# Attention pairs in a hybrid block: where the keys' sums, the two-group scores and the weighings stand in the order of the engines

## The chip, the cores and the metric

The kernel runs on one core of a Trainium2 chip. The metric is the device time of one execution in microseconds (us). A core has several engines, each with its own instruction order, which wait for one another through semaphores: TensorE (PE, matrix products), VectorE (DVE), ScalarE (ACT), GpSimd (POOL), and SyncE (SP), whose queue issues most of the transfers.

## The reference

Two layers on 512 tokens of width 1024, in float32: one dilated attention mixer and one mLSTM mixer, each followed by a feed-forward part. The change is in the attention (and, by one address, in a projection of the mLSTM). Cut to that:

```
xn = rms_norm(x, g)
proj = (xn @ w_in)                      # 3 groups x (q, k, v) x 8 heads of 128
for (window, dilation) in ((128, 1), (512, 4), (2048, 16)):     # groups 0, 1, 2
    q, k = rope(q) * scale, rope(k)     # only the first 32 of the 128 dimensions are turned
    s = q @ k^T within blocks of 128 and the block before, masked
    o, lse = softmax(s) @ v, log-sum-exp of s
o = sum over groups of softmax(lse) * o
out = o @ w_out
```

## The kernel before

The heads are worked on in four pairs (`pr` 0 to 3; tiles `a0...` to `a3...`), and each pair has three groups g0, g1, g2. `qk_unit` makes the queries and keys of one pair and group (256 columns each) by seven products in the order P1, P5, P6, P2, P7, P3, P4, in the manner of a fast matrix multiplication: sums of input halves (`S`, `S3`, `S4`) against differences of weight quarters (`less`, L958, on VectorE), and sums of the results. A product is 24 matmuls of 128x256. Float32 accuracy comes from splitting each weight chunk into a high part (`..._h`, cast on ScalarE, L239) and a low part (`..._l`, a subtraction on VectorE, L241); the matmuls go high, high, low for every quarter of the chunk, so that the first two matmuls of a product need only the high part and the third needs the low part. `Feed` issues the splits ahead of the products that use them; `feed.pop` hands out one chunk and issues (`fill`) the next.

After its product, `finish` reads the accumulators: bank copies on ScalarE (`vu`, L1007 after P5 and L1010 after P6; `u` from `c11`, L1045), copies of queries (L1022) after P2 and P4, keys' sums on VectorE (`a.g_k`, L1028) after P7 and P3, and packings of the 32 turned rows (`rot`, L990) on ScalarE. P7 and P4 add to the same accumulator `u`, so that P4 can start only when the keys' sum after P7 has read it. After P4 the rope follows on VectorE (L627 to L636), and the turned rows are copied back by ScalarE (L650) and, after g2, for the keys by POOL (L641).

Meanwhile the previous pair's attention is placed between the products: scores of group 0 (`scores0`, L729, with masked maxima on VectorE, L735), scores of groups 1 and 2 together (`both_groups`, 32 matmuls L791, eight maxima L795), exponentials on ScalarE (L814), the joint weights of the three groups (`joint`, to the factors `cf`, L855), then `weigh(0)` and `weigh(1)`, which scale the 15 probability blocks of each head in eight instructions (L863 on ScalarE, L865 on VectorE), `transposes(i)` (turnings: 2.17 us on VectorE, L878, and four DMAs on POOL's queue, L881), `bring(i)` (one DMA, L886) and `values(i)`.

What sets the order: the program is written out in one order, and each engine then gets its part through a scheduler that may interchange independent instructions by priority. Ticks (`advance`, `defer`) place the work of the previous pair: `RUN_AT` gives the tick of the two-group scores, of the seven steps of `rest` (joint, weigh 0, transposes 0, bring 0, weigh 1, transposes 1, bring 1), of the values and of the loads; `FIRST_AT` holds for the attention of pair 0, that runs in pair 1. `None` in `rest` puts a step behind g1's P7 (`behind_seventh`). `run` lets a step stand ahead; `behind(fn, engine=E)` issues it behind the last instruction so far of that engine. `ahead_of_splits` and `ahead_of_casts` name the instruction behind which the next low parts and casts go. `late` and `run_late` hold low parts back so that they are issued among the score maxima. `TOKENS` is the pair of offsets, inside padded tiles, of the high and low parts of weights for the projections of tokens (`mv`, L330).

Of the kernel before, what the change touches and what calls it, by code (L numbers as in the profile page):

```python
# [24 lines left out]
HEADS = 8  # L25
# [8 lines left out]
C2 = float(np.float32(np.uint32(np.float32(TWO_PI - C1).view(np.uint32) & 0xFFFFF000).view(np.float32)))  # L34
C3 = float(np.float32(TWO_PI - C1 - C2))
SCORES0_AT = 7
RUN_AT = (1, (4, 4.5, 5, 7, 7, 8, 9), (14.4, 15.4), (4, 5, 4))
PRODUCTS_FROM = 1
FIRST_AT = (2, (4, 4.5, None, 7, 7, 8, 9)) + RUN_AT[2:]
LAST_AT = (2, (3,), (), (4, 4, 4))  # L40
STACK_AT = (9, 11, 15, 17)
HEAD_AT = ((9, 10, 12), (10, 11, 13), (12, 13, 15), (13, 14, 16), (15, 16, 18), (16, 17, 19), (18, 19, 21),
           (19, 20, 21))
LAST_OUTPUTS = {6: 22, 7: 23}
W_BUFS = 3
PAD, WIDE, NARROW, TOKENS = 64, (0, 0), (16, 48), (48, 16)
SPLITS = [(0, 0), (0, 1), (1, 0)]


# [27 lines left out]
def tile_hybrid_dilated_attn_mlstm(  # L77
# [66 lines left out]
    def defer(n, fn):  # L144
        later.append((tick[0] + n, next(order), fn))
# [63 lines left out]
    ahead_of_splits = [None]  # L209
# [91 lines left out]
    class Feed:  # L301
# [4 lines left out]
        def __bool__(self):  # L306
            return bool(self.ready or self.plan)

        def pop(self, _=0):
            whl = self.ready.pop(0) if self.ready else self.plan.pop(0)()  # L310
            self.fill(self.ahead)
            return whl

        def fill(self, n):
# [110 lines left out]
    with ExitStack() as actx:  # L425
# [257 lines left out]
        def attention_pair(pr, qks):  # L683
# [35 lines left out]
            def scores0(q, k):  # L719

                inner = True
                for i in range(2):
                    for b2 in range(2):
                        sp = score_bank(i, "%ss0" % nm)
                        o, parts = 0, []
                        for b in (2 * b2, 2 * b2 + 1):
                            lo_ = max(b - 1, 0) * P
                            w = (b + 1) * P - lo_
                            nc.tensor.matmul(sp[:, o:o + w], q[:, i, b * P:(b + 1) * P],  # L729
                                             k[:, i, lo_:lo_ + w], start=True, stop=True)  # L730
                            parts.append((b, o, w))
                            o += w
                        for b, o, w in parts:
                            pb = max(2 * b - 1, 0)
                            nc.vector.tensor_tensor_reduce(  # L735
                                p0[i][:, pb:pb + w // P, :].rearrange("p a b -> p (a b)"),
                                sp[:, o:o + w], mask_band[:, 2 * P - w:], 1.0, -3e38,
                                op0=ALU.add, op1=ALU.max, accum_out=own[:, 0, 0, i, b:b + 1])
                    if inner:
                        behind(negate, 0, i, engine=DVE)  # L740
                        if i and pr:
                            held_exps.append(lambda i=i: exponentials(0, i, False))
                        else:
                            if i:
                                feed.fill(3)
                            exponentials(0, i, False)
                        run_late(i)
                ahead_of_splits[0] = last_on(DVE)

                def exps():  # L750
                    for i in range(2):
                        exponentials(0, i)
                if inner:
                    ahead_of_casts[0] = last_on(ACT)
                else:
                    defer(1, lambda: behind(exps, engine=ACT))
# [101 lines left out]
            def weigh(i):  # L858
                cf4 = weight[0]

                def times(blk, f):
                    if i and pr < HEADS // 2 - 1:
                        nc.scalar.activation(blk, blk, AF.Copy, scale=f)  # L863
                    else:
                        nc.vector.tensor_scalar(blk, blk, f, None, op0=ALU.mult)  # L865
                for b in range(4):
                    pb = max(2 * b - 1, 0)
                    blk = p0[i][:, pb:2 * b + 1, :].rearrange("p a b -> p (a b)")
                    times(blk, cf4[:, 0, i, b:b + 1])
                for c in range(4):  # L870
                    blk = p12[i].rearrange("p (g c) k -> p c g k", g=2)[:, c]
                    times(blk, cf4[:, 1, i, c:c + 1])
# [50 lines left out]
            return (lambda: (places(), scores0(*qks[0])), scores12, rest, values, load_values,  # L923
                    value_tiles, bring, second)

        postponed, behind_seventh = [], []

        QK_ORDER = ("P1", "P5", "P6", "P2", "P7", "P3", "P4")
        four_k = lambda t: t.rearrange("p (k n) -> p k n", k=4)
# [51 lines left out]
        def qk_unit(pr, g, qk, then=None):  # L981
# [57 lines left out]
            for n, name in enumerate(QK_ORDER):  # L1039
                key = target[name]  # L1040
                if name in ("P1", "P5"):
                    acc[key] = acc_tile(nm + key)
                if name == "P5":
                    acc["u"] = acc_tile(nm + "u")
                    nc.scalar.activation(acc["u"], acc["c11"], AF.Copy)  # L1045
                    if g:
                        ahead_of_casts[0] = last_on(ACT)
                    feed.fill(feed.ahead + 1)
                whl = feed.pop()
                with fenced():  # L1050
                    for m in range(2):
                        for k in range(4):
                            for a, b in SPLITS:
                                if name in ("P1", "P2", "P4"):
                                    x_ = pair[b][k + 4 * (name != "P1")][:, HALF * (name == "P4"):HALF * (1 + (name == "P4"))]
                                else:
                                    x_ = sum_part(name, b, k)
                                nc.tensor.matmul(acc[key][:, m * HALF:(m + 1) * HALF], whl[a][:, k, m * P:(m + 1) * P], x_,
                                                 start=(name in ("P1", "P5") and m == 0 and k == 0 and (a, b) == SPLITS[0]),
                                                 stop=(m == 1 and k == 3 and (a, b) == SPLITS[-1]), skip_group_check=True)  # L1060
                finish(name)
                if g == 1 and name == "P7":
                    while behind_seventh:
                        behind(behind_seventh.pop(0), engine=DVE)
                if pr == 0:
                    if g == 1:
                        if n == 0:
                            renew(range(4, 8))
                        elif n < 3:
                            sum_of("S%d" % (n + 2))  # L1070
                        elif n == 6:
                            back = rope(qk, rot, False)
                            defer(1, lambda: behind(back, engine=ACT))
                            for key, hf in (("W11", 1), ("W12", 0), ("W12", 1), ("W22", 0), ("W22", 1)):
                                behind(load_block, 0, key, hf, engine=mybir.EngineType.SP)
                    elif n == 6:
                        postponed.append(lambda: rope(qk, rot, False)())
                    if n in (1, 5):
                        advance()
                    continue  # L1080
                if g == 2 and n == 2:
                    feed.ahead = 2
                if n == 6:
                    with behind_scores() if g == 2 else nullcontext():
                        back = rope(qk, rot, g == 0)
                    if g == 0:
                        defer(1, lambda: back(True))
                    elif g == 2:
                        ahead_of_splits[0] = last_on(DVE)
                        back(True)  # L1090
                        ahead_of_casts[0] = last_on(ACT)
                    else:
                        defer(1, lambda: behind(back, engine=ACT))
                if g == 2 and n == 5:
                    late[0] = last or by_products(pr + 1, 0)
                    feed.fill(feed.ahead + 1)
                    late[0] = False
                if n in (1, 3, 5, 6):
                    advance()
                if n == 6 and then is not None:  # L1100
                    then()
                if n:
                    feed.fill(feed.ahead + 1)
# [289 lines left out]
        def follow(todo, at):  # L1393
            scores12_, rest, values, load = todo[1:5]
            for g in range(3):
                defer(at[3][g], lambda g=g: load(g))
            defer(at[0], lambda: run(scores12_ if at is not LAST_AT else lambda: scores12_((2,))))
            for n, fn in zip(at[1], rest):
                if n is None:
                    behind_seventh.append(fn)  # L1400
                else:
                    defer(n, lambda fn=fn: run(fn) if fn is rest[0] else fn())
            for i in range(len(at[2])):
                defer(at[2][i], lambda i=i: run(lambda: values(i)))
# [1172 lines left out]
```

## Time and profile before

| quantity | value |
|---|---|
| median of 3 runs | 1349.94 us (1349.56 to 1349.94) |
| profiled execution | 1350.34 us, span 1348.6 us |
| TensorE busy | 1329.1 us (99%) |
| VectorE busy | 1131.8 us (84%) |
| ScalarE busy | 812.8 us (60%) |
| POOL busy | 196.6 us (15%) |
| the four attention pairs in the span | about 40 to 400 us |

The span goes from the first to the last instruction; the profiled execution's own time includes what lies around it. A row of a timeline reads: start in us, duration in us, engine, line, operation, tiles written and read, shape, number of instructions in the row, and in brackets the engine's idle time before it with what ended it. Buffer numbers and the product's number are left out in the rows, so that `a3g0P_h` is any high part of pair 3, group 0.

### The profile page before, as it was taken

What the parts mean: (1) busy time and instruction counts of PE and PEld (TensorE: products, weight loads), DVE (VectorE), ACT (ScalarE), POOL (GpSimd) and SP (SyncE); (2) the same over time, 40 slices, a digit from 0 to 9 for tenths busy, and PEclk for the clock granted to TensorE, in tenths of its full rate; (3) what the DMA queues carried; (4) which work ended last, traced back from release to release, by engine and by line L of the source; (5) the groups of instructions that cost most, each with busy time, mean ns of one, the idle gap of its engine ahead of it and who ended that gap; (6) DMA issues with size and microseconds to landing.
All of it is one profiled execution on the core that took longest, in us unless ns stands there. A gap on an engine that the chain in (4) does not pass through costs nothing. (4 is left out here: it accounts for less than half of the span.)

```text
span 1348.6 us, 23346 instructions
## 1 busy us (share of the span) xinstructions
PE 1329.1 (99%) x9100; PEld 1219.9 (90%) x9100; DVE 1131.8 (84%) x1787; ACT 812.8 (60%) x1303; POOL 196.6 (15%) x272
## 2 busy tenths in 40 slices
PE   9999999999999999999999999999999999999997
PEld 7898899999998889999999998898888999999886
DVE  7988789799876399888888899898858988997887
ACT  6676577667674255555577464795534555558855
POOL 3000013141412001000010110122200202112113
PEclk9999999999999999999999999999999999999999
DMA  9354244555676357334362743324343535447863
GB/s 302 129 180 155 80 141 149 164 175 154 185 267 192 128 148 175 107 123 126 125 157 79 172 129 89 100 64 125 95 121 98 130 128 173 141 139 172 190 172 102
DMA packets 141270, 194.90 MB, mean 145 GB/s; under 512 B 9028, under 2 KB 106116, under 8 KB 141160
## 3 DMA queue, kind: packets, MB, share of 16 engines
q1 hardware_dynamic: 120128, 140.73, 33.3%
q0 software_dynamic: 19808, 52.48, 16.1%
q8 instruction: 71, 1.16, 0.4%
q10 hardware_dynamic: 1224, 0.21, 0.1%
q14 instruction: 39, 0.32, 0.1%
HBM read 167.30 MB, written 22.54 MB: 141 GB/s over the span
## 5 line engine op out<-in xcount | busy, mean ns | idle before, releaser
L1803 POOL DMA_DIRECT2D f0S<-in_ffn_w_out_dram x10 | 8.7, 875 | 245.0 <-DVE f0hid L1719 161.8
L2366 POOL DMA_DIRECT2D hD<-hB x32 | 20.7, 654 | 109.4 <-DVE hB L2363 109.2
L1827 POOL DMA_DIRECT2D f1T<-in_ffn_w_out_dram x15 | 17.8, 1186 | 86.1 <-ACT f1T L1830 40.5
L276 PE MATMUL mo<-n_h,mo_k_h 128*128 128x512 f32 x64 | 25.4, 397 | 0.0
L276 PE MATMUL mo<-n_h,mo_k_l 128*128 128x512 f32 x64 | 25.2, 394 | 0.0
L276 PE MATMUL awo<-ao_h,awo_k_h 128*128 128x512 f32 x64 | 25.2, 393 | 0.0
L276 PE MATMUL mo<-n_l,mo_k_h 128*128 128x512 f32 x64 | 25.1, 393 | 0.0
L276 PE MATMUL mwo<-yo_l,mwo_k_h 128*128 128x512 f32 x64 | 25.1, 392 | 0.0
L276 PE MATMUL mqk<-n_h,mqk_k_h 128*128 128x512 f32 x64 | 25.1, 392 | 0.0
L276 PE MATMUL mwo<-yo_h,mwo_k_l 128*128 128x512 f32 x64 | 25.1, 392 | 0.0
L276 PE MATMUL mqk<-n_l,mqk_k_h 128*128 128x512 f32 x64 | 25.1, 392 | 0.0
L276 PE MATMUL f0j<-n_h,f0j_h 128*128 128x512 f32 x64 | 25.0, 391 | 0.0
L276 PE MATMUL f1j<-n_h,f1j_h 128*128 128x512 f32 x64 | 25.0, 391 | 0.0
L276 PE MATMUL mwo<-yo_h,mwo_k_h 128*128 128x512 f32 x64 | 25.0, 391 | 0.0
L276 PE MATMUL mqk<-n_h,mqk_k_l 128*128 128x512 f32 x64 | 25.0, 391 | 0.0
L276 PE MATMUL awo<-ao_h,awo_k_l 128*128 128x512 f32 x64 | 25.0, 391 | 0.0
L276 PE MATMUL awo<-ao_l,awo_k_h 128*128 128x512 f32 x64 | 25.0, 390 | 0.0
L276 PE MATMUL f0j<-n_h,f0j_l 128*128 128x512 f32 x64 | 24.9, 390 | 0.0
L276 PE MATMUL f1j<-n_h,f1j_l 128*128 128x512 f32 x64 | 24.9, 390 | 0.0
L276 PE MATMUL f0j<-n_l,f0j_h 128*128 128x512 f32 x64 | 24.9, 389 | 0.0
L276 PE MATMUL f1j<-n_l,f1j_h 128*128 128x512 f32 x64 | 24.9, 389 | 0.0
L241 DVE TENSOR_TENSOR v1P_l<-v1W,v1P_h 128x1024 fp32r<-128x1024 f32 x14 | 17.1, 1223 | 9.2 <-ACT v1P_h L239 9.1
(2746 smaller groups left out, 5993.4 us busy)
## 6 DMA issues: line engine op xcount, KB each, us to landing
f0j_w<-in_ffn_w_in_dram SPq DMA_DIRECT2D x17, 512.0 KB, 6.0
f1j_w<-in_ffn_w_in_dram SPq DMA_DIRECT2D x17, 512.0 KB, 6.6
f1T<-in_ffn_w_out_dram POOLq DMA_DIRECT2D x15, 512.0 KB, 7.4
f0hid<-in_ffn_w_in_dram SPq DMA_DIRECT2D x9, 512.0 KB, 5.1
f1hid<-in_ffn_w_in_dram SPq DMA_DIRECT2D x9, 512.0 KB, 5.1
v0W<-in_attn_w_in_dram SPq DMA_DIRECT2D x8, 512.0 KB, 8.2
v1W<-in_attn_w_in_dram SPq DMA_DIRECT2D x8, 512.0 KB, 4.3
awo_k_w<-in_attn_w_out_dram SPq DMA_DIRECT2D x8, 512.0 KB, 4.0
```

What stands on the lines that cost most here:

```text
L241: nc.vector.tensor_tensor(lo[:, :n], raw[:, :n], hi[:, :n].bitcast(F32), op=ALU.subtract)
L276: nc.tensor.matmul(acc, whl[a][:, k, m * P:(m + 1) * P], pairs[b][kk], start=(kk == 0 and (a, b) == SPLITS[0]), stop=(kk == nk - 1 and (a, ...
L1803: nc.gpsimd.dma_start(t, src[1][:, ks], accum_op=ALU.add)
L1827: nc.gpsimd.dma_start(view(to), weight_rows(hk * UNITS + u, n), accum_op=ALU.add)
L2366: nc.gpsimd.dma_start(hD[k // 4].rearrange("(b i) x -> i b x", i=R)[:, :, c0:c0 + R], t[R * a_:R * (a_ + 1)])
```

## The change

Six things change.

1. The two-group scores of the previous pair go behind P6 of g0 instead of behind P5, in pairs 2 and 3 (`RUN_AT[0] = None`).
2. `transposes(0)` goes behind g1's P7 in all pairs (in pair 1 it already did), and `weigh(1)` right behind the bank copy of g1's P6 on ScalarE (`-1`).
3. After P7 and P3 of g1 in pairs 1 to 3 the keys' sum is written ahead of the next splits and of the turnings (`sums_first`: `feed.pop` without `fill`).
4. `weigh(0)` of pair 0 moves from VectorE to ScalarE, where 16 weighings then stand in a row in pair 1.
5. At the end of pair 3 one low part is no longer issued among the score maxima of its first half (`run_late(0)`).
6. `TOKENS` becomes (48, 48): the low parts of the mLSTM's token weights lie at another offset.

```diff
-RUN_AT = (1, (4, 4.5, 5, 7, 7, 8, 9), (14.4, 15.4), (4, 5, 4))
+RUN_AT = (None, (4, 4.5, None, 7, -1, 8, 9), (14.4, 15.4), (4, 5, 4))
-FIRST_AT = (2, (4, 4.5, None, 7, 7, 8, 9)) + RUN_AT[2:]
+FIRST_AT = (2, (4, 4.5, None, 7, -1, 8, 9)) + RUN_AT[2:]
-PAD, WIDE, NARROW, TOKENS = 64, (0, 0), (16, 48), (48, 16)
+PAD, WIDE, NARROW, TOKENS = 64, (0, 0), (16, 48), (48, 48)
...
-        def pop(self, _=0):
+        def pop(self, fill=True):
             whl = self.ready.pop(0) if self.ready else self.plan.pop(0)()
-            self.fill(self.ahead)
+            if fill is not False:
+                self.fill(self.ahead)
...
-                        run_late(i)
+                        if i or pr < HEADS // 2 - 1:
+                            run_late(i)
...
-                    if i and pr < HEADS // 2 - 1:
+                    if (i or pr == 0) and pr < HEADS // 2 - 1:
                         nc.scalar.activation(blk, blk, AF.Copy, scale=f)
...
-                whl = feed.pop()
+                sums_first = pr > 0 and g == 1 and name in ("P7", "P3")
+                whl = feed.pop(not sums_first)
...
                 finish(name)
+                if g == 0 and name == "P6":
+                    while scores_behind_sixth:
+                        scores_behind_sixth.pop()()
+                if g == 1 and name == "P6":
+                    while behind_sixth:
+                        behind(behind_sixth.pop(), engine=ACT)
+                if sums_first:
+                    ahead_of_splits[0] = last_on(DVE)
                 if g == 1 and name == "P7":
                     while behind_seventh:
                         behind(behind_seventh.pop(0), engine=DVE)
+                if sums_first:
+                    feed.fill(feed.ahead)
...
-            defer(at[0], lambda: run(scores12_ if at is not LAST_AT else lambda: scores12_((2,))))
+            if at[0] is None:
+                scores_behind_sixth.append(lambda: run(scores12_))
+            else:
+                defer(at[0], lambda: run(scores12_ if at is not LAST_AT else lambda: scores12_((2,))))
             for n, fn in zip(at[1], rest):
                 if n is None:
                     behind_seventh.append(fn)
+                elif n < 0:
+                    behind_sixth.append(fn)
```

What it does to the engines' orders is shown at three places. The names carry their buffer numbers here, and the product's number where it has one; the lines of the changed kernel are one to three higher.

First, ScalarE in pair 1, from the bank copy after g1's P6 on. Before (`a0p0` and `a0p1` are the probabilities of the two heads of pair 0):

```order
L1010 ACTIVATE a1g1vu_2134<-a1g1u_2101 128x512
L239 ACTIVATE a1g1P4_h_2168<-a1g1W21_1920 128x1024
L863 ACTIVATE a0p1_1708<-a0p1_1708,a0cf_2034 128x128
L863 ACTIVATE a0p1_1708<-a0p1_1708,a0cf_2034 128x256 x3
L990 ACTIVATE rot_2198<-a1g1c11_2068 32x512
L1022 ACTIVATE a1g1_q_2066<-a1g1c11_2068 128x2x256
L239 ACTIVATE a1g2P1_h_2201<-a1g2W11_2074 128x1024
L863 ACTIVATE a0p1_1708<-a0p1_1708,a0cf_2034 128x2x128 x4
L990 ACTIVATE rot_2198<-a1g1_k_2067 32x512
L239 ACTIVATE a1g2P5_h_2239<-a1g2W11_2074 128x1024
L990 ACTIVATE rot_2198<-a1g1_k_2067 32x512
```

Now:

```order
L1012 ACTIVATE a1g1vu_2134<-a1g1u_2101 128x512
L239 ACTIVATE a1g1P4_h_2176<-a1g1W21_1920 128x1024
L865 ACTIVATE a0p0_1707<-a0p0_1707,a0cf_2034 128x128
L865 ACTIVATE a0p0_1707<-a0p0_1707,a0cf_2034 128x256 x3
L865 ACTIVATE a0p0_1707<-a0p0_1707,a0cf_2034 128x2x128 x4
L865 ACTIVATE a0p1_1708<-a0p1_1708,a0cf_2034 128x128
L865 ACTIVATE a0p1_1708<-a0p1_1708,a0cf_2034 128x256 x3
L865 ACTIVATE a0p1_1708<-a0p1_1708,a0cf_2034 128x2x128 x4
L992 ACTIVATE rot_2206<-a1g1c11_2068 32x512
L1024 ACTIVATE a1g1_q_2066<-a1g1c11_2068 128x2x256
L239 ACTIVATE a1g2P1_h_2209<-a1g2W11_2074 128x1024
```

The weighings of the first head (`a0p0`), which were VectorE's, and all of the second now stand between P4's high part and the copies after P2; g2's P1 high part stands behind sixteen weighings instead of four.

Second, VectorE in pair 3 at g0, around the low part of P6 (`ISA` rows on `a2s12` are the maxima of the two-group scores). Before:

```order
L636 TENSOR_TENSOR rot_3339<-rot_3339 128x512
L958 TENSOR_TENSOR a3g0W11_3217<-a3g0W22_3288,a3g0W11_3217 128x1024
L958 TENSOR_TENSOR a3g0W12_3254<-a3g0W22_3288,a3g0W12_3254 128x1024
L795 ISA a2p0_3408,a2own_2595<-a2s12_3554,acst_109 128x2x128
L795 ISA a2own_2595 128x1
L241 TENSOR_TENSOR a3g0P6_l_3473<-a3g0W11_3217,a3g0P6_h_3472 128x1024
```

Now:

```order
L637 TENSOR_TENSOR rot_3339<-rot_3339 128x512
L960 TENSOR_TENSOR a3g0W11_3217<-a3g0W22_3288,a3g0W11_3217 128x1024
L960 TENSOR_TENSOR a3g0W12_3254<-a3g0W22_3288,a3g0W12_3254 128x1024
L241 TENSOR_TENSOR a3g0P6_l_3473<-a3g0W11_3217,a3g0P6_h_3472 128x1024
L241 TENSOR_TENSOR a3g0P2_l_3488<-a3g0W21_3346,a3g0P2_h_3487 128x1024
L241 TENSOR_TENSOR a3g0P7_l_3523<-a3g0W12_3254,a3g0P7_h_3522 128x1024
L960 TENSOR_TENSOR a3g0W21_3346<-a3g0W21_3346,a3g0W11_3217 128x1024
L241 TENSOR_TENSOR a3g0P3_l_3555<-a3g0W22_3288,a3g0P3_h_3554 128x1024
L797 ISA a2p0_3408,a2own_2595<-a2s12_3585,acst_109 128x2x128
```

P6's low part, and those of P2, P7 and P3, stand ahead of all maxima; before, the first maximum stood ahead of P6's.

Third, VectorE in pair 3 at g1, from P4's low part on. Before:

```order
L241 TENSOR_TENSOR a3g1P4_l_3950<-a3g1W21_3627,a3g1P4_h_3949 128x1024
L878 STREAM_TRANSPOSE a2pB_3911<-a2p0_3408 128x15x4x32
L241 TENSOR_TENSOR a3g2P1_l_3983<-a3g2W11_3845,a3g2P1_h_3982 128x1024
L1028 TENSOR_TENSOR a3g1_k_3848<-a3g1u_3875,a3g1vu_3908 128x2x256
L958 TENSOR_TENSOR a3g2W11_3845<-a3g2W12_3882,a3g2W11_3845 128x1024
L958 TENSOR_TENSOR a3g2W12_3882<-a3g2W22_3922,a3g2W12_3882 128x1024
L241 TENSOR_TENSOR a3g2P5_l_4014<-a3g2W11_3845,a3g2P5_h_4013 128x1024
L1028 TENSOR_TENSOR a3g1_k_3848<-a3g1p5_3874,a3g1vu_3908 128x2x256
```

Now:

```order
L241 TENSOR_TENSOR a3g1P4_l_3951<-a3g1W21_3627,a3g1P4_h_3950 128x1024
L1030 TENSOR_TENSOR a3g1_k_3848<-a3g1u_3875,a3g1vu_3908 128x2x256
L880 STREAM_TRANSPOSE a2pB_4013<-a2p0_3408 128x15x4x32
L241 TENSOR_TENSOR a3g2P1_l_3984<-a3g2W11_3845,a3g2P1_h_3983 128x1024
L1030 TENSOR_TENSOR a3g1_k_3848<-a3g1p5_3874,a3g1vu_3908 128x2x256
L960 TENSOR_TENSOR a3g2W11_3845<-a3g2W12_3882,a3g2W11_3845 128x1024
L960 TENSOR_TENSOR a3g2W12_3882<-a3g2W22_3915,a3g2W12_3882 128x1024
L628 STREAM_SHUFFLE rot_3980<-rot_3980 128x512
L241 TENSOR_TENSOR a3g2P5_l_4022<-a3g2W11_3845,a3g2P5_h_4021 128x1024
```

The keys' sum after P7 (the first L1028, now L1030) moves ahead of the turnings and of g2's P1 low part, and the sum after P3 ahead of the two differences and of P5's low part. On ScalarE the eight second-head weighings of this pair stand in one row between the bank copy after P6 and P4's high part; before, they stood behind that high part, four before and four behind the copies after P2 and g2's P1 high part.

The order of POOL and of SP's transfers around these places is the same in both kernels.

More of the change, by code (lines that the diff above doesn't have):

```diff
@@ L924, in attention_pair @@
                     value_tiles, bring, second)
-        postponed, behind_seventh = [], []
+        postponed, scores_behind_sixth, behind_sixth, behind_seventh = [], [], [], []
         QK_ORDER = ("P1", "P5", "P6", "P2", "P7", "P3", "P4")
```

## The prediction

> **What bounds the kernel now.** I read the shares first, then TensorE's waits, then the busy time of the stretches that the change touches, and last the timeline of each engine there.
>
> The page gives the shares; the cores' view gives the granted clock:
>
> ```profile
> PE 1329.1 (99%) x9100; PEld 1219.9 (90%) x9100; DVE 1131.8 (84%) x1787; ACT 812.8 (60%) x1303; POOL 196.6 (15%) x272
> core 0: 1348.6 us, clock 0.999
> ```
>
> TensorE is idle for 1348.6 − 1329.1 = 19.5 us of the span. The change removes no matmul, so that idle time is all that an order can win. Its waits, costliest first:
>
> ```profile
> PE a3g1u L1058 <- DVE a3g_k L1028: 1.4, 1, 1.4
> PE a1s L791 <- POOL a1g_k L641: 1.4, 1, 1.4
> PE a2g1u L1058 <- DVE a2g_k L1028: 0.8, 1, 0.8
> PE a1g2u L1058 <- ACT a1g2vu L1010: 0.7, 1, 0.7
> ...
> PE a1g1u L1058 <- DVE a1g_k L1028: 0.7, 1, 0.7
> ...
> PE a3s L771 <- DVE a3own L735: 0.5, 1, 0.5
> ```
>
> Three of them (1.4 + 0.8 + 0.7 = 2.9) are the keys' sums ahead of P4, one is the copy of keys by POOL ahead of the two-group scores, one a bank copy, one the last scores. The engines' load in pair 2 around g1 and g2 (second number TensorE, fourth VectorE, fifth ScalarE):
>
> ```profile
> 275.00:310.00 35.00, 33.61 (x292) 33.05 (x290) 33.69 (x49) 25.60 (x42) 12.63 (x19) 1.00 0.60 186
> ```
>
> In 275 to 310 VectorE is busy 33.69 of 35 us, as much as TensorE. Whatever makes VectorE stand idle there is not made good until the stretch ends. That is the view on which I decide.
>
> **Part 1: two-group scores behind P6 (pairs 2 and 3, g0).** No instruction is added; 32 matmuls and 8 reductions swap places with P6. Pair 3, rows picked from the engines' timelines, one engine after the other (start, duration, both in us), as in the fences below:
>
> ```profile
> 323.82 2.76 DVE L958 TENSOR_TENSOR a3g0W<-a3g0W,a3g0W 128x1024 f32<-128x1024 f32 x2
> 327.19 1.22 DVE L241 TENSOR_TENSOR a3g0P_l<-a3g0W,a3g0P_h 128x1024 fp32r<-128x1024 f32 x1
> 325.31 1.06 ACT L239 ACTIVATE a3g0P_h<-a3g0W 128x1024 fp32r<-128x1024 f32 x1
> 324.04 3.02 POOL L641 COPY a2g_k<-rot 32x512 f32<-32x512 f32 x2 [5.28 <-DVE rot L636]
> 325.08 3.73 PE L791 MATMUL a2s<-a2g_k,a2g_q 128*128 128x128 f32 x32
> 328.57 0.48 PE L1058 MATMUL a3g0u<-S,a3g0P_h 128*128 128x256 f32 x2
> ```
>
> P5 ends at 325.08 and the scores fill TensorE until 328.57, 3.49 us. Under that cover P6's two weight differences (to 326.58), its high part (to 326.37) and its low part (to 328.41) are made. After the change P6 itself is wanted at 325.08. Its first two matmuls need the high part, the third the low part. The low part loses only the 0.6 us of one reduction ahead of it: it starts at 326.6 and ends at 327.8. The third matmul would have run at 325.3, so about 2.4 us are lost, and the scores come 2.4 later than they would have. The cover was the scores, and it is gone. To this comes 0 to 1.0: the turnings of the second half land later (below), and first scores wait for their buffer. I take 0.5; together **+2.9** (2.4 to 3.4).
>
> In pair 2 the same happens, but here the scores did stall:
>
> ```profile
> 250.32 0.61 PE L791 MATMUL a1s<-a1g_k,a1g_q 128*128 128x128 f32 x4
> 252.35 3.39 PE L791 MATMUL a1s<-a1g_k,a1g_q 128*128 128x128 f32 x28 [1.42 <-POOL a1g_k L641]
> 255.50 0.48 PE L1058 MATMUL a2g0u<-S,a2g0P_h 128*128 128x256 f32 x2
> 250.62 2.76 DVE L958 TENSOR_TENSOR a2g0W<-a2g0W,a2g0W 128x1024 f32<-128x1024 f32 x2
> 253.67 1.26 DVE L241 TENSOR_TENSOR a2g0P_l<-a2g0W,a2g0P_h 128x1024 fp32r<-128x1024 f32 x1
> ```
>
> From 250.32 to P6's start at 255.50 are 5.18 us for 3.49 of scores: 1.69 are won. P6's low part can start at 253.4 (250.62 + 2.76) instead of 253.67 and end at 254.6, while its third matmul is wanted at 250.55: 4.0 lost if all else stood. The turnings of the second half, which now come earlier, end a wait of VectorE ahead of this place about 1.05 earlier, so 3.0. I take 3.0 − 1.69 = **+1.3**; with no gap it would be −1.7, with the whole gap +2.3.
>
> A rule bears on this place. The Trainium skill, page "SBUF — State Buffer", section "Who interferes with whom", says that a VectorE instruction with two SBUF inputs contends with a GpSimd instruction that reads SBUF, and calls the shared port an exclusive lock. By it P6's low part, now beside POOL's copy, would stand until that ends at 327.06, and the sum would be 0.4 higher, 8.9 instead of 8.5. The trace agrees only in part: the two differences beside POOL's copies took 2.76 together, so they ran, neither blocked for the 1.5 us of one copy.
>
> **Parts 2 to 4: g1 into g2.** In pairs 2 and 3 the eight weighings of the second half go to ScalarE in one piece behind the bank copy of P6, ahead of P4's high part. Pair 3:
>
> ```profile
> 359.68 1.60 ACT L863 ACTIVATE a2p<-a2p,a2cf 128x128 f32<-128x128 f32 x4 [0.30 <-DVE a2cf L855]
> 362.17 1.21 DVE L241 TENSOR_TENSOR a3g1P_l<-a3g1W,a3g1P_h 128x1024 fp32r<-128x1024 f32 x1
> 366.50 0.68 DVE L1028 TENSOR_TENSOR a3g_k<-a3g1u,a3g1vu 128x512 f32<-128x512 f32 x1
> 367.10 2.46 DVE L958 TENSOR_TENSOR a3g2W<-a3g2W,a3g2W 128x1024 f32<-128x1024 f32 x2
> 367.32 0.36 PE L1058 MATMUL a3g1u<-xa_h,a3g1P_h 128*128 128x256 f32 x1 [1.43 <-DVE a3g_k L1028]
> 373.30 0.50 PE L1058 MATMUL a3g2p<-S,a3g2P_h 128*128 128x256 f32 x2 [0.26 <-ACT a3g_q L1022]
> 381.58 0.28 PE L1058 MATMUL a3g2u<-S3h,a3g2P_h 128*128 128x256 f32 x1
> ```
>
> Eight weighings at 0.39 (1.60 for four, overlapping) run from 359.68 to 362.78, the high part of P4 (1.05) to 363.83. VectorE has nothing else in its order and stands from 362.2 to 363.8: 1.6 us idle that it did not have. Then low part to 365.0, sum to 365.7, and P4 starts at 365.75 instead of 367.32: the stall of 1.4 is gone. But the 2.17 us of turnings, the low part of P1, the second sum (done 369.5), two differences (2.46), one turn of the rope (0.73) and P5's low part follow: that low part ends at 373.6, where P5 started in the profile at 373.30. The 1.6 won at P4 are lost by P5, and what is still to do on VectorE (P6's and P2's low parts) is 1.9 later. At P7 I get 382.85 against 381.58: **+1.3** (−0.5 to +2.2). Pair 2 by the same chain: weighings start at 286.70, P4's high part moves by 2.3, VectorE idles 1.75, P4 starts 1.4 earlier, P7 0.8 later: **+0.8** (−1.0 to +1.8). The turnings' DMAs on POOL keep their order; they go 2.5 us later and nothing but the buffer above asks for them soon.
>
> In pair 1 the first half's eight weighings move from VectorE to ScalarE too:
>
> ```profile
> 211.98 1.60 ACT L863 ACTIVATE a0p<-a0p,a0cf 128x128 f32<-128x128 f32 x4 [1.67 <-DVE a0cf L855]
> 213.49 0.57 ACT L990 ACTIVATE rot<-a1g1c 32x512 f32<-32x512 f32 x1
> 213.97 0.57 ACT L1022 ACTIVATE a1g_q<-a1g1c 128x512 f32<-128x512 f32 x1
> 214.45 1.04 ACT L239 ACTIVATE a1g2P_h<-a1g2W 128x1024 fp32r<-128x1024 f32 x1
> 213.00 2.42 DVE L865 TENSOR_SCALAR a0p<-a0p,a0cf 128x128 f32<-128x128 f32 x8
> 219.36 1.18 DVE L958 TENSOR_TENSOR a1g2W<-a1g2W,a1g2W 128x1024 f32<-128x1024 f32 x1
> 220.46 0.68 DVE L1028 TENSOR_TENSOR a1g_k<-a1g1p,a1g1vu 128x512 f32<-128x512 f32 x1
> 220.31 0.28 PE L1058 MATMUL a1g2c<-xa_h,a1g2P_h 128*128 128x256 f32 x1
> 233.51 0.39 PE L1058 MATMUL a1g2u<-S3h,a1g2P_h 128*128 128x256 f32 x1 [0.74 <-ACT a1g2vu L1010]
> ```
>
> Sixteen in a row at 0.39 take 6.2: 211.98 to 218.2. Two copies at 0.48 bring g2's P1 high part to 219.16 to 220.20 (now 214.45), its low part to 221.4. TensorE, without the 0.67 stall, wants P1 at 219.6. VectorE is relieved of 2.42 but waits about 4 us for that high part. With the second sum it is done at 222.0, and the difference of 1.2 that already lay behind it at 221.1 is still to do: 0.9 + 1.2 = 2.1 late. Four copies of turned rows, which now stand ahead of P7's high part on ScalarE, add the rest: P7 at 236.4 against 233.5, less a little at the next scores: **+2.7** (0 to 3).
>
> **Parts 5 and 6.** At the end of pair 3 a low part moves behind the score reductions; their wait of 0.5 goes and nothing asks for the low part for 6 us: **−0.55**. The new address of the mLSTM token weights' low parts changes no instruction. Their 192 matmuls and those of a product:
>
> ```profile
> 848.00:908.00 60.00, 23.75 (x192) 23.24 (x192) 1.00 0.31 84
> 322.36 0.39 PE L1058 MATMUL a3g0p<-S,a3g0P_h 128*128 128x256 f32 x2
> ```
>
> are 123.7 ns apiece against 2.72 / 24 = 113.3 (P5 from 322.36 to 325.08). At best 192 × 10.4 ns = 2.0 are won, at worst I allow the same lost; nothing in the trace leans to a side: **0**.
>
> **Sum.** 2.7 + 1.3 + 0.8 + 2.9 + 1.3 − 0.55 + 0 = +8.45 us. The profiled execution took 1350.34 (span 1348.6 and 1.7 around it), 0.4 over the median of 1349.94; it would come to 1358.8, and the median, which I forecast, to 1358.4. This case's own range is 1353 to 1362.5: the ends above, which no cause drives all to one side, halved on the low side.
>
> **Rivals.** First, faster: the stalls go and nothing takes their place, 2.9 + 1.4 + 0.7 + 0.5 = 5.5 less, up to 1 us kept back by P6: 1344.4 to 1345.5. It decides at P4's high part: if ScalarE finishes the weighings before VectorE comes to P4's low part, VectorE does not idle and the 1.6 won at P4 stays. For it speaks that ScalarE is busy only 25.6 of 35 us; against it that the factors come at 359.6, just where VectorE and ScalarE are both wanted. Chance 0.17.
>
> Second, no change: the idle time of VectorE is real but slack before P7 takes it (pairs 2 and 3 at 0 instead of +2.1, pair 1 at −0.7, the stall that goes), and of P6's gaps 2.4 + 0.5 remains: 1349.94 + 2.9 − 0.7 − 0.55 = 1351.6; without the 0.5 and with the 1.69 won in pair 2, 1349.4. That is within 0.2% (2.7 us, about what a measurement of this kernel tells from no change). Chance 0.09.
>
> Third, the clock. A gap of 2.4 us is longer than any idle time of these stretches (1.43), and if the granted clock fell after one, the next products would take 5.4 instead of 2.72: one or two such places on top of the forecast, 1361.1 to 1363.8. Against it: clock 0.999 with gaps of 1.4. Chance 0.04. The Trainium skill, page "TensorE: Matmul & The Clock Gate", section "What's actually happening", sets an idle window of about 3.4 us for this, which my gaps do not reach; no run here shows where it lies.
>
> The forecast keeps 0.70. Faster 0.17, within 0.2% 0.09, slower 0.70 + 0.04 = 0.74. The range, 1346.0 to 1363.0, leaves out the first rival's time (1344.4 to 1345.5) and holds its milder outcomes; with the forecast's own tails that leaves about 0.18 outside.
>
> **What would show it.** In the new profile: no wait of P4 on the keys' sums; P6 of pair 3's g0 broken behind its second matmul for about 2.4 us by its low part; VectorE idle 1.6 us ahead of P4's low part in pairs 2 and 3, released by ScalarE's cast; ScalarE with 16 weighings from 212 to 218 and P1 of pair 1's g2 late. I am wrong if VectorE has no such idle time, or if P6's low part ends before P5 does.

## The result, and the profile after

The changed kernel takes 1362.41 us (median of 5 runs, 1360.84 to 1364.27) against 1349.94 before (1349.56 to 1350.86, 5 runs beside it): a ratio of 1.0091 with a 95% interval from 1.0076 to 1.0106, 12.5 us slower. It is inside the forecast range (1346.0 to 1363.0), on the forecast side, but 4 us above the forecast point of 1358.4 and close to the range's upper end: two of the five runs lie above it. The profiled execution took 1363.26 us, with a span of 1361.5.

The page's shares and the granted clock of the changed kernel:

```profile
PE 1334.7 (98%) x9100; PEld 1223.2 (90%) x9100; DVE 1129.7 (83%) x1779; ACT 815.8 (60%) x1311; POOL 196.2 (14%) x272
core 0: 1361.5 us, clock 0.995
```

TensorE's idle time went from 19.5 to 26.8 us (1361.5 − 1334.7). The span grew by 12.9; the other 5.6 us are TensorE's busy time, although no matmul was added. Of these, 2.5 are matmuls at half clock (the table below); the rest was not taken apart. The mean granted clock is 0.995 instead of 0.999. TensorE's waits, costliest first:

```profile
PE a1g2p L1061 <- ACT a1g2P_h L239: 2.9, 2, 2.4
PE a3g0u L1061 <- ACT a3g0P_h L239: 2.1, 1, 2.1
PE a2g0u L1061 <- ACT a2g0P_h L239: 2.1, 1, 2.1
...
PE a3g0u L1061 <- DVE a3g0P_l L241: 0.8, 1, 0.8
PE a1g2c L1061 <- DVE a1g2P_l L241: 0.8, 1, 0.8
PE a2g0u L1061 <- DVE a2g0P_l L241: 0.8, 1, 0.8
```

The three waits on keys' sums (2.9) and the one on POOL (1.4) are gone, as the change sets out. What took their place is the split of weights: high parts from ScalarE and low parts from VectorE, at P6 of g0 (pairs 2 and 3) and in g2 of pair 1. P6 of pair 3's g0 in the engines' timelines:

```profile
330.61 2.76 DVE L960 TENSOR_TENSOR a3g0W<-a3g0W,a3g0W 128x1024 f32<-128x1024 f32 x2
333.80 1.22 DVE L241 TENSOR_TENSOR a3g0P_l<-a3g0W,a3g0P_h 128x1024 fp32r<-128x1024 f32 x1 [0.42 <-ACT a3g0P_h L239]
331.41 1.27 ACT L651 ACTIVATE a2g_q<-rot 32x512 f32<-32x512 f32 x2
332.71 1.06 ACT L239 ACTIVATE a3g0P_h<-a3g0W 128x1024 fp32r<-128x1024 f32 x1
333.82 0.50 PE L1061 MATMUL a3g0u<-S,a3g0P_h 128*128 128x256 f32 x2 [2.08 <-ACT a3g0P_h L239]
335.07 0.58 PE L1061 MATMUL a3g0u<-S,a3g0P_l 128*128 128x256 f32 x1 [0.76 <-DVE a3g0P_l L241]
```

P5 ends at 331.74, and P6 waits 2.08 us for its high part and 0.76 for its low part. The single matmul that follows took 0.58 us; behind the same wait in pair 2 it took 0.39. The reason is in the stretches around the two P6 (first number length, second TensorE busy; the number behind the engines' is the granted clock):

```profile
251.50:256.00 4.50, 2.86 (x26) 2.66 (x24) 3.83 (x4) 4.28 (x12) 2.94 (x2) 1.00 0.00 0
256.00:260.00 4.00, 2.81 (x22) 2.61 (x23) 2.00 (x2) 4.00 (x11) 0.00 (x0) 1.00 0.00 0
331.50:334.50 3.00, 0.74 (x5) 0.34 (x3) 2.58 (x3) 2.95 (x8) 2.29 (x2) 1.00 0.00 0
334.50:338.50 4.00, 3.42 (x17) 3.43 (x18) 2.42 (x3) 4.00 (x10) 0.00 (x0) 0.57 0.00 0
```

In pair 2 the clock stays at 1.00 through the gap; in pair 3 it falls to about half behind it, and P6's last 22 matmuls take 4.0 us instead of 2.6. The same happens once more behind the 2.37 us gap in pair 1's g2.

The start times of the products in the traces of before and after, subtracted stage by stage, give where the time went. The column on half clock is what the last 22 matmuls of the product behind the gap took longer than at full clock (first start to last start 3.62 instead of 2.49 in pair 1, 3.90 instead of 2.50 in pair 3). The last column is a kernel shown below (`both_gaps_filled`), in which the clock fell nowhere in these stages:

| stage | forecast | changed kernel | of it half clock | no half clock |
|---|---|---|---|---|
| pair 1, g1 and g2 to the next scores | +2.7 | +4.1 | 1.1 | +2.9 |
| pair 2, g0 | +1.3 | +1.7 | 0 | +1.8 |
| pair 2, g1 and g2 to P7 | +0.8 | +0.9 | 0 | +0.9 |
| pair 3, g0 | +2.9 | +4.8 | 1.4 | +3.4 |
| pair 3, g1 and g2 to P7 | +1.3 | +1.5 | 0 | +1.5 |
| end of pair 3 | −0.55 | −0.6 | 0 | −0.7 |
| sum | +8.45 | +12.4 | 2.5 | +9.8 |

### The profile page after: what moved, and what is told of

It is laid out like the page before. It is cut to its first block, busy times and chain, and to the rows that moved or that the text cites. A ratio compares the mean times of both kernels' runs of the same rounds, so it can differ in the third digit from the quotient of the medians.

```text
span 1361.5 us, 23341 instructions
## 1 busy us (share of the span) xinstructions
PE 1334.7 (98%) x9100; PEld 1223.2 (90%) x9100; DVE 1129.7 (83%) x1779; ACT 815.8 (60%) x1311; POOL 196.2 (14%) x272
## 3 DMA queue, kind: packets, MB, share of 16 engines
q8 instruction: 71, 1.16, 0.3%
```

## The experiments

Each was run 4 to 11 times beside the kernel before, whose median was 1349.8 to 1350.0 in all of them.

**Part 1 undone** (`scores_behind_p5`).

```diff
-RUN_AT = (None, (4, 4.5, None, 7, -1, 8, 9), ...
+RUN_AT = (1, (4, 4.5, None, 7, -1, 8, 9), ...
```

> The changed kernel with part 1 undone: two-group scores behind P5 again, all else as changed. Theory (P6 waits because the scores no longer cover its split): the gaps of 2.8 us ahead of P6's third matmul in pairs 2 and 3 go, and with them the half-clock stretch behind the one in pair 3; the wait for POOL's copy of keys (1.4) comes back in pair 2. Against the 1362.4 of the changed kernel 1.6 + 3.2 = 4.8 less, and 1.5 more where the clock had fallen: 1356 to 1358. Rival (the lateness is made in pairs 1 to 3 between g1 and g2, and P6's gap only shows it): the gap moves elsewhere, 1361 to 1363.

Measured: 1353.85 us (1352.56 to 1355.85), ratio 1.0030 [1.0018, 1.0041], 8.6 less than the changed kernel and 2 below the expected range. No wait of P6 in g0 is left:

```profile
328.74 0.61 PE L793 MATMUL a2s<-a2g_k,a2g_q 128*128 128x128 f32 x4
329.68 3.39 PE L793 MATMUL a2s<-a2g_k,a2g_q 128*128 128x128 f32 x28 [0.33 <-POOL a2g_k L642]
332.82 0.48 PE L1061 MATMUL a3g0u<-S,a3g0P_h 128*128 128x256 f32 x2
```

P6 starts when the scores end. Pair 3's g0 costs 0.6 instead of 4.8, and pair 2's g0 costs 1.6 less than before instead of 1.7 more: the wait for POOL did not come back in pair 2, which I had counted (1.4); TensorE comes there 4.1 late from pair 1, POOL's copy perhaps less so. The theory holds, and part 1 is the dearest part of the change.

**Part 1 alone on the kernel before** (`part1_alone`; the same lines of the diff of part 1, nothing else).

> The kernel before with part 1 alone: the two-group scores behind P6 of g0 in pairs 2 and 3. Theory (P6's split is no longer covered): P6 waits 2.5 to 2.9 us in both pairs, less the 1.4 to 1.7 that the scores no longer wait for POOL in pair 2: +1.3 to 1.7 and +2.4 to 3.3, and 0 to 1.5 where the clock falls in one g0: 1353.7 to 1356.2, against 1349.8 to 1350.0 before. Rival (in the changed kernel the gap was made by the lateness out of g1 and g2 before it): less than 1 us slower, 1350 to 1351.

Measured: 1357.39 us (1355.93 to 1358.59), ratio 1.0053 [1.0040, 1.0065]: 7.4 slower, 1.2 above the expected range. P6 of pair 2 and pair 3:

```profile
251.60 0.50 PE L1058 MATMUL a2g0u<-S,a2g0P_h 128*128 128x256 f32 x2 [2.38 <-ACT a2g0P_h L239]
253.38 0.38 PE L1058 MATMUL a2g0u<-S,a2g0P_l 128*128 128x256 f32 x1 [1.27 <-DVE a2g0P_l L241]
329.34 0.50 PE L1058 MATMUL a3g0u<-S,a3g0P_h 128*128 128x256 f32 x2 [1.17 <-ACT a3g0P_h L239]
331.11 0.39 PE L1058 MATMUL a3g0u<-S,a3g0P_l 128*128 128x256 f32 x1 [1.27 <-DVE a3g0P_l L241]
```

The gaps are there without any of the other parts, so the rival falls: they are not made by lateness from ahead. In pair 2 the two waits make 3.65 us and the clock falls behind them; the g0 of pair 2 costs 4.1 and that of pair 3 3.0.

**Part 4 undone** (`weigh0_on_vector`).

```diff
-                    if (i or pr == 0) and pr < HEADS // 2 - 1:
+                    if i and pr < HEADS // 2 - 1:
```

> The changed kernel with part 4 undone: pair 0's first eight weighings on VectorE again, all else as changed. Theory (sixteen weighings in a row on ScalarE keep back the high part of g2's P1 in pair 1): that high part comes about 3.1 us earlier, VectorE idles less than 1 us instead of about 4, and pair 1 costs 0 to 1.5 instead of 4.1: 1358.5 to 1361. Rival (ScalarE has slack, the loss of pair 1 is VectorE's order alone): within 1 us of 1362.4.

Measured: 1359.52 us (1358.70 to 1361.48), ratio 1.0072 [1.0059, 1.0085], 2.9 less than the changed kernel. ScalarE in pair 1, of the changed kernel:

```profile
211.74 6.30 ACT L865 ACTIVATE a0p<-a0p,a0cf 128x128 f32<-128x128 f32 x16 [1.67 <-DVE a0cf L857]
218.89 1.04 ACT L239 ACTIVATE a1g2P_h<-a1g2W 128x1024 fp32r<-128x1024 f32 x1
219.97 1.23 DVE L241 TENSOR_TENSOR a1g2P_l<-a1g2W,a1g2P_h 128x1024 fp32r<-128x1024 f32 x1 [2.81 <-ACT a1g2P_h L239]
```

and of this kernel:

```profile
210.80 3.20 ACT L865 ACTIVATE a0p<-a0p,a0cf 128x128 f32<-128x128 f32 x8 [1.67 <-DVE a0cf L857]
214.86 1.05 ACT L239 ACTIVATE a1g2P_h<-a1g2W 128x1024 fp32r<-128x1024 f32 x1
```

With eight weighings in the row the high part of P1 starts 4.06 us behind the first weighing instead of 7.15, so 3.1 earlier, as expected. VectorE no longer waits for it (2.81 before its low part in the changed kernel), and pair 1 costs 0 instead of 4.1. In this profile the clock was half for 6.8 us in pair 3's g0, whose cost rose from 4.8 to 6.3; that fits a whole that gained less than the 4.1 of its stage.

**weigh(1) back at its tick** (`weigh1_at_tick`).

```diff
-RUN_AT = (None, (4, 4.5, None, 7, -1, 8, 9), ...
+RUN_AT = (None, (4, 4.5, None, 7, 7, 8, 9), ...
-FIRST_AT = (2, (4, 4.5, None, 7, -1, 8, 9)) + ...
+FIRST_AT = (2, (4, 4.5, None, 7, 7, 8, 9)) + ...
```

> The changed kernel with weigh(1) at its tick 7 again instead of right behind the bank copy of P6, all else as changed. Theory (in pairs 2 and 3 the eight weighings ahead of P4's high part make VectorE idle 1.6 us, in pair 1 they keep back P1's high part): P4's high part stands ahead of seven of the weighings, VectorE no longer idles there, 0.9 + 1.5 less in pairs 2 and 3 and 2 to 4 less in pair 1: 1356 to 1359.5. Rival (VectorE's sequence of low parts alone sets P7, the idle time is slack): pairs 2 and 3 unchanged, 1359.5 to 1362.

Measured: 1361.43 us (1361.07 to 1361.87), ratio 1.0085 [1.0071, 1.0099]: a miss, only 1.0 less than the changed kernel. Pair 1 did cost 3.1 less (1.1 instead of 4.1), but two things stood against that. The granted clock fell in three stretches of this profile instead of two, one of them in pair 2's g0, which cost 3.6 instead of 1.7. And g1 and g2 of pairs 2 and 3 cost 1.1 and 1.05, against 0.9 and 1.5. VectorE in pair 3, here:

```profile
371.96 1.21 DVE L241 TENSOR_TENSOR a3g1P_l<-a3g1W,a3g1P_h 128x1024 fp32r<-128x1024 f32 x1
374.61 1.23 DVE L241 TENSOR_TENSOR a3g2P_l<-a3g2W,a3g2P_h 128x1024 fp32r<-128x1024 f32 x1 [1.44 <-ACT a3g2P_h L239]
375.75 0.68 DVE L1030 TENSOR_TENSOR a3g_k<-a3g1u,a3g1vu 128x512 f32<-128x512 f32 x1
376.35 2.17 DVE L880 STREAM_TRANSPOSE a2pB<-a2p 128x1920 f32<-128x1920 f32 x1
```

VectorE does not stand any more ahead of P4's low part, but 1.44 us ahead of P1's. The scheduler had put that low part ahead of the sum and the turnings, and its high part is not ready. So the idle time had moved, and the run told nothing of whether it was slack.

**Three parts undone** (`three_parts_undone`: parts 1 and 4 undone and weigh(1) at its tick, as in the three diffs above).

> The changed kernel with the scores behind P5, weigh(1) at tick 7 and pair 0's first weighings on VectorE, so that of the change stay: keys' sums ahead of the splits, transposes(0) behind P7, the last low part and the address. Theory (the stretch is bound by VectorE, an earlier sum only changes which product waits): no gain from the sums, 0.55 from the end of pair 3 and 0.5 from the address: 1348.5 to 1350. Rival (the sums' stalls of 2.9 us vanish once nothing holds P4's low part back): 1345.5 to 1347.5.

Measured: 1351.2 us (1350.26 to 1352.22), ratio 1.0008 [0.9999, 1.0018]: 1.2 above the expected range, and the interval just includes no change. The early sums gain nothing, and in the trace there is some loss: g1 and g2 of pairs 2 and 3 cost 1.1 each, with the same 1.4 us of VectorE's idle time ahead of P1's low part.

**The same, without VectorE's idle time** (`no_vector_idle`). One chunk fewer is split ahead after P6 and P2 of g1, so that the scheduler has P1's low part behind the sum and the turnings:

```diff
                 if n:
-                    feed.fill(feed.ahead + 1)
+                    feed.fill(feed.ahead + (0 if pr > 1 and g == 1 and name in ("P6", "P2") else 1))
```

> The kernel with three parts undone (1351.2), and in pairs 2 and 3 one chunk fewer split ahead after P6 and P2 of g1, so that VectorE's order from P4's low part on is that of the changed kernel (low part, sum, turnings, P1's low part, sum, two differences) but P4's high part does not stand behind eight weighings. Theory (what the early sums win is lost because VectorE stands idle 1.4 us for a high part, in that kernel for P1's, in the changed one for P4's): without that idle time P7 of g2 comes 0.2 later than in the kernel before instead of 1.1, in both pairs: 1349.2 to 1350.2. Rival (it is the order behind the sums, with the rope ahead of P6's low part, not the idle time): P7 still 1 later, 1351 to 1351.7.

Measured: 1349.08 us (1348.59 to 1351.32), ratio 0.9994 [0.9985, 1.0003], 2.1 less than with the idle time. VectorE in pair 3, of the changed kernel and then of this one:

```profile
371.04 2.40 DVE L867 TENSOR_SCALAR a2p<-a2p,a2cf 128x128 f32<-128x128 f32 x8
375.23 1.23 DVE L241 TENSOR_TENSOR a3g1P_l<-a3g1W,a3g1P_h 128x1024 fp32r<-128x1024 f32 x1 [1.79 <-ACT a3g1P_h L239]
376.37 0.68 DVE L1030 TENSOR_TENSOR a3g_k<-a3g1u,a3g1vu 128x512 f32<-128x512 f32 x1
376.98 2.17 DVE L880 STREAM_TRANSPOSE a2pB<-a2p 128x1920 f32<-128x1920 f32 x1
```

```profile
358.88 2.40 DVE L867 TENSOR_SCALAR a2p<-a2p,a2cf 128x128 f32<-128x128 f32 x8
361.19 1.22 DVE L241 TENSOR_TENSOR a3g1P_l<-a3g1W,a3g1P_h 128x1024 fp32r<-128x1024 f32 x1
362.86 0.69 DVE L1030 TENSOR_TENSOR a3g_k<-a3g1u,a3g1vu 128x512 f32<-128x512 f32 x1 [0.45 <-PE a3g1u L1061]
363.47 2.17 DVE L880 STREAM_TRANSPOSE a2pB<-a2p 128x1920 f32<-128x1920 f32 x1
```

The order from P4's low part to the second pair of differences is the same in both; only the 1.79 us for the high part are gone, for 0.45 that the sum waits for P7. P7 of g2 then comes 0.4 earlier (pair 2) and 0.2 later (pair 3) than in the kernel before, instead of 0.9 and 1.5 later. In the kernels with part 1 or part 4 undone these stages still cost 1.1 and 0.9 (pair 2) and 1.5 (pair 3), so those parts do not make the difference. That is the test that the run with weigh(1) at its tick had missed: the idle time is the cost. And even without it the early sums win next to nothing, since VectorE then has the same work to do up to P6's low part.

**Parts 5 and 6 alone on the kernel before** (`end_and_address`; their two lines of the diff).

> The kernel before with parts 5 and 6 alone: the last low part of pair 3 no longer among the first half's maxima, and the other address. Theory: the end of pair 3 wins 0.5 to 0.8, the projection of tokens 0.3, nothing else moves: 1348.7 to 1349.4 where the kernel before has 1349.9 to 1350.0. Rival (the end's wait only moves to the next projection): 1349.6 to 1350.2.

Measured: 1348.81 us (1348.26 to 1350.08), ratio 0.9995 [0.9986, 1.0004]. The median is 1.0 lower, in the expected range, but the interval includes no change. In the trace the end of pair 3 is 0.8 shorter, and the address shows in the matmuls of `mv` (minimum, median and maximum in ns; before, and with the new address in the changed kernel):

```profile
L330 PE MATMUL mv<-mv_k_h,n_h x64: 278/281/384, 850.2 to 906.4; 128*128 128x256 f32 x64
L331 PE MATMUL mv<-mv_k_h,n_h x64: 276/276/384, 862.6 to 918.4; 128*128 128x256 f32 x64
```

But TensorE waits longer at the next products: ahead of `m1nb` 0.9 us instead of 0.5, in this kernel and in the changed one, and the weight load for `m2num` behind it 0.6 instead of 0.2. What the matmuls of `mv` win is lost there again.

**The first gap filled** (`gap_filled`): 18 matmuls whose result nobody reads, behind P5 of g0 in pairs 2 and 3.

```diff
                 finish(name)
+                if pr > 1 and g == 0 and name == "P5":
+                    fill_ps = ps.tile([P, 512], F32, tag="t", name=nm + "fill", bufs=1)
+                    for i in range(18):
+                        with tc.issue_after(last_on_pe()):
+                            nc.tensor.matmul(fill_ps[:, :256], whl[0][:, i % 4, :P], x_, start=True, stop=True)
+                    fence[0] = last_on_pe()
```

> The changed kernel with 18 extra matmuls of 128x256 (a high part of P5 again, into an accumulator that nobody reads) behind P5 of g0 in pairs 2 and 3, where TensorE otherwise waits 2.1 us for P6's high part: 2.04 us of TensorE work in each gap. Theory (the granted clock falls to half behind such a gap and P6 then runs at 183 ns per matmul instead of 120): the gaps cost what they cost, but the granted clock stays at 1.00 in both g0, and a run loses no 1.5 us there: 1360 to 1361.5, at most 1 us spread more than from pair 1's own gap. Rival (P6's matmuls are slow for another reason, and the clock is a side effect): P6 of pair 3 stays at 4.0 us, and the time at 1362 to 1364.

Measured: 1363.24 us (1361.45 to 1364.85), ratio 1.0098 [1.0084, 1.0112]. A miss: in the profile the clock fell in pair 3's g0 again, although TensorE had worked through the first gap. The stretch from the gap on:

```profile
331.50:335.50 4.00, 2.68 (x22) 2.28 (x20) 4.00 (x3) 3.95 (x10) 2.97 (x2) 1.00 0.00 0
335.50:339.50 4.00, 3.80 (x19) 3.80 (x20) 2.93 (x4) 3.57 (x6) 0.00 (x0) 0.57 0.00 0
```

TensorE was idle 1.3 of 4.0 us here, 1.26 of it ahead of P6's third matmul.

**Both gaps filled** (`both_gaps_filled`): besides, 8 such matmuls between P6's second and third matmul, with P6's own high part.

> The changed kernel with the 18 extra matmuls behind P5 of g0 (pairs 2 and 3) and 8 more between P6's second and third matmul, 0.9 us where TensorE waits 0.8 to 1.3 for the low part. Filling the first gap alone left the fall of the clock in pair 3's g0: 1.4 us of idle time in the 3.4 us ahead of it remained. Theory (the clock falls by how little TensorE did in the last 3.4 us): with under 0.6 us of idle time left no fall in either g0, P6's last 22 matmuls at 113 to 120 ns, and a run 1360.5 to 1362, without the 1364.5 of some runs before. Rival (the fall follows the restart after any wait, or the kind of data, not the idle share): half clock in pair 3's g0 again in the profile, and runs at 1361.5 and 1364.5 side by side.

Measured: 1361.97 us (1360.49 to 1362.34), ratio 1.0085 [1.0072, 1.0099]. The same stretch:

```profile
329.50:332.00 2.50, 2.45 (x23) 2.25 (x21) 2.22 (x3) 2.45 (x6) 2.44 (x2) 1.00 0.00 0
332.00:335.50 3.50, 3.50 (x29) 3.44 (x30) 1.96 (x2) 3.50 (x10) 0.13 (x1) 1.00 0.00 0
```

Here the clock is 1.00, and P6's last 22 matmuls take 2.62 us. The profile of this run (1360.49 us) has no half clock in the attention; it is the last column of the table. The runs with the first gap filled lie in two groups (1361.5 and 1362.0, 1364.5 and 1364.9), those with both filled between 1360.5 and 1362.3. So in these profiles the fall in pair 3 goes with idle time ahead of P6. One profile does not settle it: in the same profile there is no fall behind pair 1's gap either, although nothing fills that gap and it is 2.40 us long; the last section comes back to this. The median is only 0.4 below that of the changed kernel, and the runs overlap. Without any fall the change still costs 9.8 in these stages.

## Why the prediction was right

The forecast said slower, by 8.45 us, for three reasons that the trace of before could show: P6 loses the scores that covered its split, VectorE is made to stand for high parts that ScalarE holds back behind weighings, and what the early sums win is lost at the next products. All three are shown.

- Part 1. Forecast 2.9 (pair 3) and 1.3 (pair 2); measured 3.4 and 1.8 without half clock. The step was right and its size too small: I let P6's high part come 1.3 us behind P5's end and the low part fix the gap at 2.4, but ScalarE came to the cast only at 332.71, behind its turned copies, so the high part alone cost 2.08, and the low part 0.76 on top.
- Part 4 and pair 1. Forecast 2.7, measured 2.9 without half clock; the sixteen weighings took 6.30 (forecast 6.2) and the high part of P1 came at 218.9 (forecast 219.2). Taking half of them away took the whole cost of the stage away.
- g1 and g2 of pairs 2 and 3. Forecast for pairs 2 and 3: VectorE's idle time 1.75 and 1.6, P7 0.8 and 1.3 later; measured 1.79 in both, and 0.9 and 1.5. P4 starts with 0.2 us of its stall left, and the gain is lost at P5, which waits for its copy of queries and its low part, and at P6, as the chain had it (PE in pair 3: P4, P5, P5's third matmul, P7):

```profile
377.20 0.36 PE L1061 MATMUL a3g1u<-xa_h,a3g1P_h 128*128 128x256 f32 x1
383.95 0.50 PE L1061 MATMUL a3g2p<-S,a3g2P_h 128*128 128x256 f32 x2 [0.83 <-ACT a3g_q L1024]
385.05 0.39 PE L1061 MATMUL a3g2p<-S,a3g2P_l 128*128 128x256 f32 x1 [0.59 <-DVE a3g2P_l L241]
394.36 0.35 PE L1061 MATMUL a3g2u<-S3h,a3g2P_h 128*128 128x256 f32 x1
```

- The end: −0.55 forecast, −0.6 to −0.8 measured. The address: taken as 0, and the matmuls of `mv` became some 5 ns of 281 shorter; all 192 keep TensorE busy for 23.06 us instead of 23.75. That is inside the allowed 2.0 to either side, and the longer waits behind them take it back.
- The clock. The step that failed. I gave 0.04 to a gap after which the granted clock falls, on the ground that gaps of 1.4 had not done it. It fell in two places of the changed kernel's profile and made 2.5 of its 12.4 us; how often it fell in the other four runs is not known. The third rival had the event right and its price too high: 2.7 a place, measured 1.1 and 1.4, since the clock stayed half for 3.4 us and not for two products' time. Its time, 1361.1 to 1363.8, holds the measured median, which the forecast's point misses by 4. The rest of the difference to the forecast, 1.35, is that five of the six terms were 0.1 to 0.5 too small.
- The faster rival said ScalarE would finish the weighings before VectorE came to P4's low part. VectorE stood 1.79 us for the cast behind them. Once the order let it not stand (the kernel without VectorE's idle time), the result was 1349.08 against 1349.76, with an interval that includes no change: the stalls of the keys' sums were gone there too, and almost nothing was won, since P5 and P6 of g2 wait for their splits there (in pair 3 they take 3.63 and 3.71 us from start to start, before 2.85 and 2.72).

The rule of the Trainium skill on the port that VectorE and GpSimd share (page "SBUF — State Buffer", section "Who interferes with whom"), weighed in the prediction, would have added 0.4. P6's low part waited for ScalarE, not for POOL, and then took its usual 1.22. The two differences beside POOL's copies took 2.76 again, 0.3 more than the two in g2 with no copy beside them (2.47). No run here shows an engine blocked for the length of a copy, and none takes the 0.3 apart.

## What to carry to other kernels

A wait that stands at the top of a list is worth what the next engine in the chain can spare: here VectorE was as busy as TensorE in the stretch, and each stall taken away came back two products later. Before moving work away from a place, ask what it covered: 3.5 us of scores hid the split of the next product's weights. And an operand's preparation on one engine (a cast) should not stand behind long work that nobody waits for yet; eight small scalings ahead of one cast made a second engine idle for 1.79 us.

## What was not expected of the hardware

After gaps in TensorE's work the granted clock fell to half. Half microseconds in which it changed, in the changed kernel and then in the one with the first gap filled (length, TensorE busy, granted clock):

```profile
235.50:236.00 0.50, 0.11 (x1) 0.63 0.78 173
239.00:239.50 0.50, 0.50 (x6) 0.95 1.11 327
334.50:335.00 0.50, 0.00 (x0) 0.62 0.00 0
338.00:338.50 0.50, 0.50 (x6) 0.97 0.00 0
```

```profile
236.50:237.00 0.50, 0.50 (x6) 0.90 0.87 207
335.50:336.00 0.50, 0.30 (x2) 0.89 0.00 0
```

A mean of 0.63 over 0.50 us says that the clock was half for the last 0.37: from 235.63 to 239.05 and from 334.62 to 338.0, 3.4 us each. The falls lie 99.0 us apart in both kernels (236.90 and 335.89 in the second). In the kernel with weigh(1) at its tick they begin at 224.24, 254.96 and 333.46, which is 30.7 and 78.5 us apart. The Trainium skill, page "TensorE: Matmul & The Clock Gate", section "What's actually happening", has a free-running window of 3413 ns; 29 of them make 99.0, and the traces agree: 9 make 30.7 and 23 make 78.5. Its rule that an idle window throttles does not fit as it stands. In the 3.41 us that end at the two falls of the changed kernel TensorE was busy for 1.30 and 1.03 us, and in those of the kernel with the first gap filled for 1.52 and 1.89. In steps of 3.41 us from the changed kernel's first fall, one stretch ends at 256.11 and holds most of pair 2's gap; TensorE was busy for 1.66 us of it, and the clock stayed. So a stretch that is idle in part is enough, and how little work it takes stays open.

The place of a gap against these steps seems to count too. A gap of 2.08 us in pair 2's g0 had a fall behind it in the kernel with weigh(1) at its tick, where the stretch that ends at the fall holds 1.16 us of work, and a gap of 2.07 had none in the changed kernel. That would also explain why pair 1's gap had no fall behind it with both gaps filled, and why runs of the changed kernel spread over 3.4 us (1360.84 to 1364.27) and those of the kernel before, in the runs beside them, over 1.3. It was not tested by itself.
